# Adaptation columns 16 to 47 as matmuls, and six convolved units whose two token halves lie in neighbouring PSUM banks

## The chip, the core and the metric

One core of a Trainium2 chip runs the whole program. Its engines work side by side, each through its own queue in order: TensorE (PE, with its weight loads PEld), VectorE (DVE), ScalarE (ACT), GpSimd (POOL) and SyncE (SP), from whose queue nearly all DMAs are issued. The metric is device time in microseconds (us); lower is better.

## The reference, cut to what matters

One layer of a decoder: 1024 tokens, width 1024, float32. A conditioning vector gives six modulation vectors; the combined projection's first columns go through a short causal convolution over the tokens.

```
mod = silu(c) @ w_ada + b_ada            # 1024 -> 6 * 1024
shift1, scale1, gate1, shift2, scale2, gate2 = split(mod, 6)
h = rms_norm(x, norm1_w) * (1 + scale1) + shift1
gq, gk, gv, gz, ga, gb, sq, sk, sv = split(h @ w_in)
q, k, v = split(silu(causal_depthwise_conv(concat(gq, gk, gv), conv_w)))   # width 4
# gated delta rule on q, k, v in chunks of 64 (a triangular solve in each), gated by gz
# sliding-window attention on sq, sk, sv
x = x + gate1 * (concat(both) @ w_out)
x = x + gate2 * ffn(rms_norm(x, norm2_w) * (1 + scale2) + shift2)
```

## The kernel before

The tokens lie along the free dimension, 128 channels on the partitions. Float32 weights and activations are split into a high and a low part, and each product of a projection is three matmuls of 128x512 (`mm3`). A *unit* is one block of 128 output columns for one half of the tokens (512 columns, one PSUM bank): 8 steps of 3 matmuls. The units of all projections form one long generator, `dense`; `fill(n)` issues its next n steps. TensorE's instructions run in the order in which the program names them. The order on the other engines comes from a scheduler, which follows the program's order and prefers what stands in `high_priority`. The order of the stage is written out by hand: `VISITS_A` and `VISITS_B` say how many dense steps stand between two visits of the other work.

**The adaptation columns.** `mod` has 48 columns of 128 values. Columns 0 to 15 (shift1 and scale1) are made at the start, ahead of the first units, from `cb`, a tile that holds silu(c) on every partition. The other 32 come later: a loop of 14 rounds (`ADA_ITER`) issues six dense steps and two columns a round, and the last four come after the visit of `v3`. A column is one load of 512 KB (`load_ada`, L247) into a slot of one of the tags b, c, d, e (two slots each), and `mod_col`: on VectorE one product with a running sum (L253), or on GpSimd a product (L256) and on ScalarE a sum (L257); then VectorE adds the bias (L259). They are used far later: the first, gate1, by the output projection.

**The convolved units.** The twelve blocks of keys, queries and values (`gk`, `gq`, `gv`) go through `conv`: ScalarE reads the bank once with the newest tap (L363), VectorE adds the three older taps, shifted by 1, 2 and 3 columns (L365). Where the second half of the tokens starts, the shifted reads need the last three columns of the first half. They are kept in `tails` (L368), and three small VectorE instructions repair columns 0 to 2 (L371). The dense banks are four: two under the tag `u`, two under `sw`, which the units take in turn (`dbank`).

**What follows.** After the loop `token_gen` makes the decays (VectorE, then `psg` and `pst` on TensorE). Each of four head pairs has three visits: sums of squares from transposes (`pst_k`, `pst_q`, L708 to L711), scaled rows (`psr_k`, L721 to L727), products (`psA`, L781 to L783). `key_gen` makes the window keys (`ps_kd`). `solve` inverts all triangles on VectorE (L817, L820). Meanwhile TensorE does the values, the window queries (`ps_sq`, with rows `psr_s`) and the gates (`ps_gz`). Then come the scan, the attention, the output projection and the FFN. Most tiles of 4 KB a partition (`cb`, the keys `kn`, the values `v`, `ktok`, `vs` and others) share one pool of six slots.

## Time and profile before

| | us |
|---|---|
| median of 3 runs (1319.52 to 1326.32) | 1319.54 |
| the profiled execution | 1316.65 |
| its span, first to last instruction | 1314.9 |
| TensorE busy | 1192.7 |
| VectorE busy | 892.6 |
| GpSimd busy | 629.4 |
| ScalarE busy | 538.8 |

Busy time is the time in which at least one instruction of the engine runs. The mean granted clock of TensorE over the span is 0.96 of full speed. Times inside the profile count from the span's start.

### The profile page before, as it was taken

The numbers are of one execution on the slowest core, as the hardware profiler recorded it, in microseconds if no ns is written. First come the engines' busy times: TensorE is split into PE (matmuls) and PEld (weight loads), VectorE is DVE, ScalarE is ACT, GpSimd is POOL, SyncE is SP. The second block draws the span as 40 slices with busy tenths as digits, with TensorE's granted clock in tenths as the row PEclk, the third lists the DMA queues.
The fourth block names the chain that finished last, engine by engine and source line by source line (L and its number), as shares of the span: only waits on it lengthen the run. The fifth ranks groups of instructions, "written<-read, shape, count | busy, mean of one in ns | idle before, by whom it ended". The sixth has DMA issues, their size and how long they took to land.

```text
span 1314.9 us, 18979 instructions
## 1 busy us (share of the span) xinstructions
PE 1192.7 (91%) x6710; PEld 974.5 (74%) x6710; DVE 892.6 (68%) x1690; ACT 538.8 (41%) x1028; POOL 629.4 (48%) x453
## 2 busy tenths in 40 slices
PE   6867697896999799997998999999999999999998
PEld 5757576684788678785786788777777888888887
DVE  7999989979724677576646416877876875546430
ACT  4373555422434777434356432222232334544430
POOL 4667344534335444344354455545455545455440
PEclk8899799898999899998899999999999999999999
DMA  8727468485639865366845625556665567775651
GB/s 326 233 85 273 144 132 227 133 229 183 199 126 205 132 113 165 106 218 216 288 157 187 207 95 203 208 200 228 212 212 201 176 217 281 250 252 195 201 168 40
DMA packets 167214, 250.62 MB, mean 191 GB/s; under 512 B 40656, under 2 KB 106448, under 8 KB 165584
## 3 DMA queue, kind: packets, MB, share of 16 engines
q1 hardware_dynamic: 157520, 241.03, 56.6%
q0 software_dynamic: 9600, 8.39, 3.9%
q8 instruction: 53, 0.87, 0.3%
q14 instruction: 41, 0.34, 0.1%
HBM read 182.89 MB, written 66.45 MB: 190 GB/s over the span
## 4 chain that ended last, share of the span: by engine, by line
PE 43%; DVE 16%; DMA 8%; issue 4%; POOL 3%; ACT 3%; SPq 0%; DVEq 0%; ACTq 0%; POOLq 0%
PE ps_P L1359 5%; PE ps_P L1358 5%; PE ps_P L1360 5%; DMA wb<-in_wgate_dram 4%; PE ps_S L1358 2%; PE ps_S L1359 2%; PE ps_S L1360 2%; PE ps_c L1358 2%; PE ps_c L1359 2%; POOL wS L193 2%; PE ps_c L1360 2%; DVE wa L1427 1%; PE ps_gz L212 1%; DMA SD<-sd 1%; DVE soltmp L817 1%
## 5 line engine op out<-in xcount | busy, mean ns | idle before, releaser
L193 POOL TENSOR_TENSOR wP<-rP,wP 128x512 fp32r<-128x512 f32 (+1 forms) x84 | 108.3, 1301 | 105.3 <-ACT wP L192 100.2
L1359 PE MATMUL ps_P<-t,wP 128*128 128x512 f32 x308 | 120.4, 391 | 0.0
L1358 PE MATMUL ps_P<-t,wP 128*128 128x512 f32 x308 | 120.4, 391 | 0.0
L1360 PE MATMUL ps_P<-t,wP 128*128 128x512 f32 x308 | 120.2, 390 | 0.0
L193 POOL TENSOR_TENSOR wS<-wa,wS 128x512 fp32r<-128x512 f32 x44 | 62.8, 1437 | 111.8 <-ACT wS L192 78.9
L1360 PE MATMUL ps_S<-T,wS 128*128 128x512 f32 x264 | 102.8, 390 | 0.3 <-POOL wS L193 0.3
L1359 PE MATMUL ps_S<-T,wS 128*128 128x512 f32 x264 | 102.9, 390 | 0.0
L1358 PE MATMUL ps_S<-T,wS 128*128 128x512 f32 x264 | 102.9, 390 | 0.0
L192 ACT ACTIVATE wP<-rP 128x512 fp32r<-128x512 f32 (+1 forms) x84 | 48.4, 590 | 77.6 <-PE ps_P L1360 49.2
L1358 PE MATMUL ps_c<-B,w 128*128 128x512 f32 x176 | 70.5, 401 | 6.1 <-ACT X L1398 6.1
L1360 PE MATMUL ps_c<-B,w 128*128 128x512 f32 x176 | 69.7, 396 | 0.0
L1359 PE MATMUL ps_c<-B,w 128*128 128x512 f32 x176 | 69.7, 396 | 0.0
L1465 ACT ACTIVATE sg<-sg 128x512 f32<-128x512 f32 x33 | 20.9, 632 | 116.0 <-DVE sg L1461 116.0
L1358 PEld LDWEIGHTS ps_P<-t,wP 128*128 128x128 f32 x308 | 57.9, 188 | 12.6
L1360 PEld LDWEIGHTS ps_P<-t,wP 128*128 128x128 f32 x308 | 57.9, 188 | 12.5
L1359 PEld LDWEIGHTS ps_P<-t,wP 128*128 128x128 f32 x308 | 57.8, 188 | 12.4
L192 ACT ACTIVATE wS<-wa 128x512 fp32r<-128x512 f32 x44 | 26.7, 624 | 94.6 <-DVE wa L1426 71.8
L1424 DVE TENSOR_TENSOR ws<-wb 128x512 f32<-128x512 f32 x22 | 23.1, 1051 | 62.1 <-DMA wb<-in_wgate_dram 54.5
L1360 PEld LDWEIGHTS ps_S<-T,wS 128*128 128x128 f32 x264 | 49.6, 188 | 11.1 <-POOL wS L193 0.7
L212 PE MATMUL ps_o<-mix,w_o 128*128 128x512 f32 x128 | 53.7, 420 | 4.2 <-ACT w_o L192 4.2
L1358 PEld LDWEIGHTS ps_S<-T,wS 128*128 128x128 f32 x264 | 49.6, 188 | 10.5
L1359 PEld LDWEIGHTS ps_S<-T,wS 128*128 128x128 f32 x264 | 49.6, 188 | 10.5
(507 smaller groups left out, 3559.4 us busy)
## 6 DMA issues: line engine op xcount, KB each, us to landing
ada<-in_ada_dram SPq DMA_DIRECT2D x48, 512.0 KB, 4.7
AD<-ops SPq DMA_DIRECT2D x11, 1536.0 KB, 5.0
rP<-SD SPq DMA_DIRECT2D x16, 704.0 KB, 5.7
sd<-in_wdown_dram SPq DMA_DIRECT2D x20, 512.0 KB, 5.3
SD<-sd SPq DMA_DIRECT2D x20, 512.0 KB, 3.9
rP<-in_wdown_dram SPq DMA_DIRECT2D x12, 704.0 KB, 5.3
XD<-X SPq DMA_DIRECT2D x22, 256.0 KB, 3.3
xu<-XD SPq DMA_DIRECT2D x22, 256.0 KB, 3.4
```

The costliest lines, as they stand in the source:

```text
L192: act.activation(out=r(hi), in_=src, func=AF.Copy)
L193: last = eng.tensor_tensor(out=r(lo), in0=src, in1=hi, op=ALU.subtract)
L212: pe.matmul(out, lhsT=r(lhs[0]), rhs=r(rhs[0]), start=first, stop=False)
L817: dve.tensor_tensor(out=tv[g], in0=bc(L[:, i, i + 1:32].unsqueeze(1), (P, i, 31 - i)), in1=bc(L[:, 0:i, i:i + 1], (P, i, 31 - i)), op=ALU. ...
L1358: pe.matmul(ps, lhsT=r(wh), rhs=r(xh), start=first and i == 0, stop=False, **kw)
L1359: pe.matmul(ps, lhsT=r(wh), rhs=r(xl), start=False, stop=False, **kw)
L1360: pe.matmul(ps, lhsT=r(wl), rhs=r(xh), start=False, stop=i == n - 1, **kw)
L1424: dve.tensor_tensor(out=s1, in0=a21, in1=a22, op=ALU.add)
L1427: dve.tensor_tensor(out=a12, in0=a12, in1=a11, op=ALU.subtract)
L1465: act.activation(out=out, in_=out, func=AF.Silu)
```

## The change

The later 32 adaptation columns become matmuls in 8 groups of four columns. All 32 loads stand ahead of the loop, from a copy of the weights laid out with the 1024 inputs on the partitions (8 blocks of 128). A group (`ada_gen`) has four steps: two of 16 float32 matmuls each, then ScalarE's copy of the bank, then four matmuls of one column and VectorE's addition of four biases at once. In each product the stationary operand is 128x32, silu(c) of one block of inputs repeated over 32 columns; the four column tiles of TensorE take the blocks k = 0..3 and then k = 4..7, so a bank holds four partial rows on partitions 0, 32, 64 and 96 (each repeated 32 times). The closing matmul of a column takes the row as stationary operand and `sel`, a column that is 1 on those four partitions, and so sums the four parts and turns the row into a column. The loop keeps its 14 rounds of six dense steps; from the fourth on, three steps of the groups follow in each. The columns behind the visit of `v3` are gone.

Six of the convolved units, `gk` 3, `gq` 3 and `gv` 0 to 3, take a tile of two neighbouring banks for both token halves. They go in pairs (first half of both, then second half of both, `two_units`), and for the second half the three shifted reads of 512 columns start 1 to 3 columns ahead of its bank, in the first half's. `tails` and the repairs are not issued for them. The four dense banks are a pool of their own that is released and opened anew at two points (`switch`): ahead of these six units as two tiles of two banks, behind them as before.

```diff
+    psd = [tc.alloc_tile_pool(name="psd0", bufs=2, space=PSUM, reuse_waits="tile")]
+    def new_banks():
+        psd[0].release()
+        psd[0] = tc.alloc_tile_pool(name=f"psd{len(psd)}", bufs=2, space=PSUM, reuse_waits="tile")
+        psd.append(None)
...
+        if tag in ("u", "sw"):
+            return psd[0].tile([P, TH], F32, tag=tag, name=name)
...
+    sel = cp.tile([P, 1], F32, name="sel")
+    pool.memset(sel, 0.0)
+    for g in range(4):
+        pool.memset(sel[32 * g:32 * g + 1], 1.0)
-    def ada_some(n, tag, eng=dve):
...
+    def ada_load(tag):
+        u = ada_next[0]
+        ada_next[0] += 1
+        adat[u] = t4(f"ada{u}", (P, KT, P), tag=tag)
+        with tc.issue_after((done["kd"] if "kd" in done else done["x"]).ins):
+            sp.dma_start(out=adat[u], in_=ada2[u - 16])
+    def ada_gen(u0, q=None):
+        ps = sm(f"ps_ada{u0}", q)
+        for m in range(2):
+            for n in (2 * m, 2 * m + 1):
+                w = adat.pop(u0 + n)
+                for k in range(KT):
+                    g = k % 4
+                    pe.matmul(ps[32 * g:32 * g + 32, n * P:(n + 1) * P], lhsT=bc(c_col[:, k:k + 1], (P, 32)), rhs=w[:, k],
+                              start=k < 4, stop=k >= 4, tile_position=(0, 32 * g))
+            yield
+        row = t2(f"ada_row{u0}")
+        act.activation(out=row, in_=ps, func=AF.Copy)
+        yield
+        for n in range(4):
+            pe.matmul(ps[:, n:n + 1], lhsT=row[:, n * P:(n + 1) * P], rhs=sel, start=True, stop=True)
+        dve.tensor_tensor(out=modc[:, u0:u0 + 4], in0=ps[:, 0:4], in1=b_ada[:, u0:u0 + 4], op=ALU.add)
+        yield
...
+        if hf == 1 and ct in wides:
+            both = wides[ct].rearrange("p a t -> p (a t)")
+            for d in (1, 2, 3):
+                dve.scalar_tensor_tensor(out=out, in0=both[:, TH - d:2 * TH - d], scalar=w[:, 3 - d:4 - d], in1=out,
+                                         op0=ALU.mult, op1=ALU.add)
+            return
...
-        if hf == 0:
+        if hf == 0 and ct not in wides:
...
-    def two_units(kinds, tags):
+    def two_units(kinds, tags, wide=False):
+        if wide:
+            for kind, p in kinds:
+                wides[CT[kind] + p] = psd[0].tile([P, 2, TH], F32, tag="w", name=f"ps_{kind}{p}")
...
-                  proj("gk", 1, (1,)), proj("gq", 1, (1,)), proj("gk", 3), proj("gq", 3),
-                  *(proj("gv", p) for p in range(4)), *(proj("sq", p) for p in range(4)), proj("gz", 0, tags=("u",)), proj("gz", 1, tags=("u",)),
+                  proj("gk", 1, (1,)), proj("gq", 1, (1,)), switch(), two_units((("gk", 3), ("gq", 3)), None, True),
+                  two_units((("gv", 0), ("gv", 1)), None, True), two_units((("gv", 2), ("gv", 3)), None, True), switch(), *(proj("sq", p) for p in range(4)), proj("gz", 0, tags=("u",)), proj("gz", 1, tags=("u",)),
...
+    adas = chain(*(ada_gen(16 + 4 * i) for i in range(8)))
+    for tag in ADA_TAGS:
+        ada_load(tag)
     for i in range(ADA_ITER):
         fill(VISITS_A[0])
-        with tc.issue_after(h_done[0].ins), tc.issue_after(h_done[1].ins):
-            ada_some(1, ADA_TAGS[2 * i], pool if i not in ADA_DVE else dve)
-            ada_some(1, ADA_TAGS[2 * i + 1])
+        for _ in range(3 if i >= 3 else 0):
+            next(adas, None)
+    run(adas)
...
-        if visit is v3:
-            for i in range(32 - 2 * ADA_ITER):
-                ada_some(1, "b", pool if i % 4 else dve)
...
-        "ada": w_ada.T.reshape(48, P, D),
+        "ada": w_ada[:, 0:2 * D].T.reshape(16, P, D),
+        "ada2": tiles(w_ada[:, 2 * D:]),
```

## Rows read from the trace of the kernel before

**Rows 1.** The page: the span and TensorE's busy time, its share and instructions.
```profile
span 1314.9 us, 18979 instructions
...
PE 1192.7 (91%) x6710; PEld 974.5 (74%) x6710; DVE 892.6 (68%) x1690; ACT 538.8 (41%) x1028; POOL 629.4 (48%) x453
```

**Rows 2.** Windows: length, busy us (PE, PEld, DVE, ACT, POOL), clock, DMA.
```profile
85.00:345.00 260.00, 200.60 (x1147) 166.35 (x1145) 240.67 (x489) 109.53 (x181) 124.96 (x61) 0.89 0.60 176
345.00:1315.00 970.00, 925.95 (x5222) 751.83 (x5222) 581.13 (x1091) 388.13 (x778) 454.15 (x346) 0.98 0.60 190
...
96.90:145.70 48.80, 41.93 (x210) 36.07 (x210) 48.37 (x76) 20.73 (x46) 32.78 (x13) 0.93 0.69 248
145.70:157.70 12.00, 0.00 (x0) 0.00 (x0) 12.00 (x33) 5.58 (x9) 2.34 (x1) 0.59 0.42 131
```

**Rows 3.** Waits of TensorE up to 440 us, longest first: total, times, longest.
```profile
PE psr_s L725 <- ACT wide_s L721: 15.0, 2, 13.4
PE psg L666 <- DVE tsc L661: 12.1, 1, 12.1
PE psr_k L725 <- ACT wide_k L721: 9.9, 2, 7.5
PE ps_gk L212 <- ACT kq L387: 8.6, 1, 8.6
...
PE ps_kd L870 <- DVE aq L783: 4.0, 1, 4.0
...
PE ps_skv L212 <- DVE qt L365: 3.7, 1, 3.7
...
PE ps_skv L212 <- DVE kn L365: 2.4, 1, 2.4
```

**Rows 4.** The tile `ada`: durations in ns, min/median/max, and its loads' landing.
```profile
L256 POOL TENSOR_TENSOR ada<-ada,cb x17: 2338/2402/3221, 85.0 to 319.8; 128x1024 f32<-128x1024 f32 x17
...
L253 DVE CUSTOM_DVE_ANT_0 ada<-ada,cb x15: 1206/1211/3451, 98.6 to 306.2; 128x1024 f32<-128x1024 f32 x15
...
DMA to landing us min/median/max: 3.3/4.7/10.2
```

**Rows 5.** VectorE's groups by line between 60 and 345 us.
```profile
L371 DVE SCALAR_TENSOR_TENSOR kn<-tails,sml,kn 128x1 f32<-128x1 f32 (+2 forms) x12 | 14.4, 1202 | 0.0
...
L371 DVE SCALAR_TENSOR_TENSOR v<-tails,sml,v 128x1 f32<-128x1 f32 (+2 forms) x12 | 9.8, 812 | 0.0
L259 DVE TENSOR_TENSOR modc<-modc,sml 128x1 f32<-128x1 f32 x32 | 9.6, 314 | 0.1
```

**Rows 6.** Timeline of VectorE, modulation of the second half: start, us, what.
```profile
85.12 5.59 DVE L332 SCALAR_TENSOR_TENSOR h<-xt,modc,h 128x512 fp32r<-128x512 f32 x2
...
91.30 0.74 DVE L332 SCALAR_TENSOR_TENSOR h<-xt,modc,h 128x512 fp32r<-128x512 f32 x1
```

**Rows 7.** Timelines of GpSimd and VectorE in the solve.
```profile
311.58 5.00 POOL L256 TENSOR_TENSOR ada<-ada,cb 128x1024 f32<-128x1024 f32 x2 [10.41 <-DVE soltmp L817]
...
312.33 2.00 DVE L820 TENSOR_TENSOR lanes<-lanes,soltmp 128x234 f32<-128x234 f32 x1
314.25 2.59 DVE L817 TENSOR_TENSOR soltmp<-lanes 128x238 f32<-128x238 f32 x1
...
319.37 0.39 DVE L820 TENSOR_TENSOR lanes<-lanes,soltmp 128x238 f32<-128x238 f32 x1
```

**Rows 8.** Timelines of TensorE: float32 matmuls, stationary size, moving size.
```profile
71.22 0.95 PE L321 MATMUL ssps<-ones,sq 128*128 128x1 f32 x8
...
247.91 2.59 PE L781 MATMUL psA<-kq,kn 64*64 64x128 f32 x64
...
445.95 1.09 PE L1170 MATMUL psO<-pT,vs 128*64 128x256 f32 x8
```

**Rows 9.** Timelines of ScalarE and VectorE: the second half of `gq` 1 read out.
```profile
171.60 0.73 ACT L363 ACTIVATE qt<-ps_gq,sml 128x512 f32<-128x512 f32 x1
...
175.85 0.73 DVE L365 SCALAR_TENSOR_TENSOR qt<-ps_gq,sml,qt 128x509 f32<-128x509 f32 x1
```

More of the change, by code (lines that the diff above doesn't have):

```diff
@@ L61, in tile_hybrid_layer @@
     ada: bass.AP,
+    ada2: bass.AP,
     wmain: bass.AP,
@@ L89, in tile_hybrid_layer @@
     psp = ctx.enter_context(tc.tile_pool(name="psp", bufs=1, space=PSUM))
-    P_BUFS = {"u": 2, "sw": 2, "q0": 1, "q1": 1, "qq": 2}
+    psd = [tc.alloc_tile_pool(name="psd0", bufs=2, space=PSUM, reuse_waits="tile")]
[3 more added lines that the diff above has]
+        psd.append(None)
+    P_BUFS = {"q0": 1, "q1": 1, "qq": 2}
     def t4(name, shape=(P, T), tag=None, dt=F32):
@@ L259, in mod_col @@
             dve.tensor_tensor(out=modc[:, u:u + 1], in0=modc[:, u:u + 1], in1=b_ada[:, u:u + 1], op=ALU.add)
+    sel = cp.tile([P, 1], F32, name="sel")
+    pool.memset(sel, 0.0)
+    for g in range(4):
+        pool.memset(sel[32 * g:32 * g + 1], 1.0)
     ada_next = [16]
-    def ada_some(n, tag, eng=dve):
-        for u in range(ada_next[0], ada_next[0] + n):
-            if "kd" in done:
-                with tc.issue_after(done["kd"].ins):
-                    load_ada(u, tag)
-            else:
-                load_ada(u, tag)
-            mod_col(u, eng)
-        ada_next[0] += n
+    def ada_load(tag):
[21 more added lines that the diff above has]
+        yield
     def rstd(ps, name):
@@ L358, in tile_hybrid_layer @@
     kns, kq, vts = {}, {}, {}
+    wides, CT = {}, {"gq": 0, "gk": 4, "gv": 8}
     def conv(ps, out, ct, hf):
@@ L366, in conv @@
                                      op0=ALU.mult, op1=ALU.add)
-        if hf == 0:
+        if hf == 0 and ct not in wides:
             dve.tensor_copy(out=tails[:, ct], in_=ps[:, TH - 3:TH])
-        else:
+        elif hf:
             for d in (1, 2, 3):
@@ L423, in proj @@
         for hf in halves:
-            ps = dbank(f"ps_{kind}{p}_{hf}", tags)
+            ps = wides[CT[kind] + p][:, hf] if CT.get(kind, 99) + p in wides else dbank(f"ps_{kind}{p}_{hf}", tags)
             yield from unit(ps, w, h_hl(hf))
@@ L595, in tile_hybrid_layer, with switch @@
         w_2 = [wunit(wmain[2], "w_gk2", parts=[t4(f"w_gk2{x}", (P, KT, P), tag="e") for x in "hl"]), wunit(wmain[6], "w_gq2")]
+    def switch():
+        new_banks()
+        yield from ()
     def skv_unit(i):
@@ L1603, in tile_hybrid_layer @@
         close_pools(len(stacks[side]), side)
+    psd[0].release()
 def kernel(**inputs):
```

## The prediction

> **What bounds the kernel now.** I read the page first. TensorE works in 1192.7 us of a span of 1314.9 [rows 1], so what can be won is its idle time, and then the question is where that lies. The windows answer it: between 85 and 345 us TensorE works 200.60 of 260 us, and in the 970 us behind them 925.95 [rows 2]. The first stretch has 59.4 us of idle time and a mean granted clock of 0.89; the second is TensorE's own and moves as a block when the first gets shorter. In the first stretch VectorE works 240.67 of 260 us [rows 2]. The view of TensorE's waits names who it waits for there: a row of the pair chains or of the window queries (`psr_s` 15.0, `psr_k` 9.9), the token sums (`psg` 12.1), a bank not yet read out (`ps_gk` 8.6, `ps_skv` 3.7 and 2.4), `ps_kd` 4.0 [rows 3]. All of them end at VectorE, directly or one ScalarE instruction behind it. So the stage is a TensorE order that stands still when VectorE is late.
>
> VectorE is late for two reasons. It does adaptation columns itself: 15 of 1.2 us and the 32 additions of their bias [rows 4, 5]. And it stands still while GpSimd does the other 17, 2.4 us each [rows 4]: `L332` takes 0.74 us alone, but two of them take 5.59 us when GpSimd's column products begin in front of them [rows 6]; in the solve, instructions of 0.39 us take 2.00 and 2.59 while the products run [rows 7]. The small `L371` repairs at the half boundary suffer most: at most three columns wide, they average 1.20 us for keys and 0.81 for values, where the shortest need 0.2 [rows 5].
>
> **What the change does to the adaptation loop (88 to 158 us).** Off VectorE, GpSimd and ScalarE goes all of it: 15 products of 1.2 us, 17 of 2.4 us, and 24 of 32 bias additions. Onto TensorE go 8 groups. A group is 32 fp32 matmuls of 128 columns, and an fp32 matmul is two instructions in the trace (the 4 matmuls of `ssps` are x8 [rows 8]), so 512 passes; then 4 matmuls of one column, 8 passes.
>
> The price of a pass: `ssps`, where each must wait for the one ahead, has 8 in 0.95 us, 0.119 each [rows 8]. The passes of a group go to four column tiles in turn. No row shows a 128x32 tile, so the bounds are: one after another, 512 x 0.119 = 61 us; four at a time, 15.2 us. The nearest rows are `psA`, 64 passes of 128 columns in 2.59 us, 0.040 each, which is three times as dense as one after another; and `psO`, where the first four passes belong to one column tile and the last four to the other, and all eight, twice as wide, end within 1.09 us [rows 8]: one after another they would need 8 x 0.24 = 1.9. So column tiles run side by side, even when the program names one tile's passes first. I take four at a time with some filling and emptying: 16 steps of 32 passes, each 8 x 0.119 + 0.1 = 1.05 us, 16.8 us. By `psA`'s rate as it stands it would be 20.5.
>
> The closing columns cost 8 x 0.95 = 7.6 us at `ssps`'s price. They wait for ScalarE's copy of the bank; in two of eight groups no dense step lies between the last product, the copy and the closing matmuls, and each of those costs a full-bank ScalarE pass (0.73 us [rows 9]) and the handing over, 0.9 by estimate: 1.8. Together TensorE takes on 16.8 + 7.6 + 1.8 = 26.2 us, and nothing hides it, because it stands in TensorE's own order.
>
> Taken away in the same loop: the wait for `psg`, 12.1 us, in which TensorE does nothing at all [rows 2, 3]. The token chain that it waits for is short VectorE work behind the columns, and in the new order some 18 dense steps and twelve adaptation steps follow its inputs. The two waits of `ps_skv`, 6.1 us [rows 3], are banks not read out because VectorE is behind. Of the 8.6 us of `ps_gk` only 4.1 go (5.59 less 2 x 0.74 [rows 6]); the modulation itself stays. The clock was granted at 0.93 over the 210 matmuls of the loop [rows 2], 14% of 48.8 us at the lower of its two levels, 1.2 GHz; with the waits gone I give back 2 us. Sum 12.1 + 6.1 + 4.1 + 2 = 24.3. The loop is therefore a draw: 26.2 - 24.3 = +1.9 us.
>
> The loads are as many and as large, on the same queue, but now TensorE's order waits for them. Each slot is refilled six columns ahead; three adaptation steps and six dense steps pass in some 5 to 7 us, so a refill has about 10 us, and a load lands in 4.7 (median) to 10.2 us [rows 4]. I take no wait, with the rival below. A load that waits on SP for its slot holds the dense units' weights behind it, as it does now; the four columns that were loaded during the solve join this queue too.
>
> **The pair chains (158 to 276 us).** Six of the twelve convolved units lose their three `L371` and the copy of the tail. By rows 5 the values' 12 cost 9.8 us, and one key unit 14.4 / 4 = 3.6, one query unit about the same: 17 us of VectorE. Half of that was standing still behind GpSimd, and will partly be met by the next instruction instead. The new reads take one operand from the sums' banks, as the main sums (`L365`, 0.73 us, rows 9) do now. Besides, `cb` is no longer held after the start, so its slot of the six-slot pool is free for a key tile whose convolution waited for one. Against it stands the new wait: a pair of units owns four banks, so at the switch the first wide unit needs the bank of the unit just ahead. That is read out 5.0 us after ScalarE begins on it (171.60 to 176.58 [rows 9]). What stands behind it on TensorE is the next pair's transposes. Within the wide units the slack falls from three units to one, some 5.5 us and the visits between. The waits to win are `psr_k` and `ps_kd`, 13.9 us [rows 3]; I take 9 of them, and 4 back for the switch: -5. Bounds: -13.9 and +5.
>
> **The solve (285 to 345 us).** Four columns leave it: one VectorE product of 1.2 us and three GpSimd ones, two of which hold VectorE for 2.00 - 0.39 and 2.59 - 0.39 [rows 4, 7]; the third at their mean, 1.9. Sum 6.9 us. TensorE waits there for `psr_s` (13.4 us at the longest of 15.0 in rows 3), which hangs on the same VectorE queue, so all of it counts: -7. The second switch, to the window queries, may cost some 5 us, but the same wait covers it.
>
> **Sum:** +1.9 - 5 - 7 = -10 us. The profiled execution took 1316.65 us (span 1314.9): 1306.6. The median of the runs is 2.9 above it, which would give 1309.5; I say 1308.
>
> **Rivals.**
> *More goes than I take.* The whole 8.6 us of `ps_gk` (4.5 more), and all of 13.9 with no wait at the switch (9 more): -24, 1295. For it: VectorE is over 90% busy and loses some 30 us there. Against it: some of these chains are latency, not load.
> *The passes start strictly in order.* Then the second pass of one tile stands in front of the next tile's first, and only two run together: 512 / 2 x 0.119 = 30.5 us, 13.7 more: 1322, no change. `psO` speaks against it; `psA`'s 0.040 lies between two and four at a time. The Trainium skill (TensorE: Matmul & The Clock Gate, Part 3: Packing small matmuls) says that matmuls start and end strictly in program order; by that rule this rival holds, and the trace's `psO` does not agree.
> *The column tiles do not overlap at full height.* The rows show two column tiles of 128 rows at once, never four. One after another they cost 61 us, 44 more: 1352, slower. It decides from 0.052 us a pass on (16.8 + 10 us over 512); above 0.065 the kernel is measurably slower.
> *Banks.* The switch in full, the same at the second switch, and a short one per wide pair: 1 + 5 + 6 = 12 more: 1320. For it: VectorE's evacuations lag in this stage. Against it: the freed slot and VectorE's relief.
> *Late loads.* If half of the eight groups find a column 3 us late (landing near 10 us): 12 more, 1320. For it: GpSimd waits for these loads today; against it: the slots are asked for earlier.
>
> **How the numbers follow.** The forecast has 0.46 (own range 1301 to 1315), more gain 0.16, strict order 0.13, no overlap 0.08, banks 0.10, late loads 0.07. 0.5%, about what can be told from no change, is 6.6 us around 1319.5. Faster: nearly all of the forecast and the bigger gain, 0.60. Slower: no overlap and the upper ends of the other three, 0.15. The rest, 0.25, is no change. The range leaves out no overlap, and the ends of the others: 1291 to 1325.
>
> **What would show it.** In the loop: some 512 passes `ps_ada`, 32 in about 1 us (1.9 would be strict order, 3.8 no overlap); no wait at `psg`; TensorE at `psg` near 158 to 160 us. VectorE below 80% between 97 and 146 us. Then `psr_k` and `ps_kd` waits smaller, a new wait of a wide unit at the first switch, and no `L371` behind the third pair of units. The solve some 7 us shorter, and the block behind 345 us unchanged in length. I am wrong if TensorE waits for `ada`, if 32 passes take over 1.7 us, or if the wide units wait for banks again and again.

## The result, and the profile after

The changed kernel takes 1333.2 us (median of 10 runs, 1327.1 to 1338.5), the kernel before on the same chip 1319.5 (10 runs, 1317.3 to 1327.7). The ratio is 1.0076, with a 95% interval of 1.0049 to 1.0103: slower, by 10 us (13.7 between the medians) where 11.5 less was forecast, and outside the range.

The profiled execution took 1327.83 us. Its page, for [rows 1]: TensorE is 31.1 us busier, VectorE 47.1 less.

```profile
span 1326.0 us, 20013 instructions
...
PE 1223.8 (92%) x7286; PEld 1001.8 (76%) x7286; DVE 845.5 (64%) x1612; ACT 523.6 (39%) x1002; POOL 595.1 (45%) x441
```

The windows of the changed kernel, cut where TensorE reaches the same work as in before: the loop from `gk` 2's second half to `psg`, the pair stage, the solve part up to the scan's first `psm`, scan and output projection, the rest. Columns as in [rows 2].

```profile
93.50:168.10 74.60, 68.89 (x787) 59.17 (x788) 26.08 (x65) 19.59 (x40) 7.08 (x3) 0.91 0.60 215
168.10:285.80 117.70, 97.64 (x669) 79.95 (x668) 95.21 (x164) 55.42 (x83) 52.99 (x24) 0.94 0.62 162
285.80:358.60 72.80, 65.19 (x301) 52.75 (x299) 60.01 (x183) 20.47 (x30) 31.28 (x21) 0.93 0.69 196
358.60:653.70 295.10, 277.63 (x2394) 225.31 (x2394) 183.66 (x564) 150.59 (x357) 124.54 (x107) 0.95 0.66 169
653.70:1326.00 672.30, 643.87 (x2784) 524.09 (x2782) 402.23 (x514) 230.58 (x414) 329.58 (x236) 0.99 0.57 194
```

The same cuts in the kernel before:

```profile
96.90:157.70 60.80, 41.93 (x210) 36.07 (x210) 60.37 (x108) 26.31 (x55) 35.12 (x14) 0.86 0.63 225
157.70:276.00 118.30, 102.09 (x669) 83.86 (x670) 104.66 (x190) 57.28 (x85) 54.30 (x25) 0.91 0.62 162
276.00:353.90 77.90, 62.11 (x302) 51.22 (x301) 68.58 (x193) 22.97 (x35) 32.30 (x23) 0.91 0.66 196
353.90:648.10 294.20, 273.04 (x2394) 221.37 (x2394) 183.60 (x566) 150.52 (x357) 124.10 (x107) 0.97 0.66 173
648.10:1314.90 666.80, 644.03 (x2785) 523.22 (x2783) 392.69 (x513) 232.83 (x414) 325.59 (x236) 0.99 0.57 196
```

Read as differences: `psg` is reached 10.4 us later, the pair stage gives back 0.6 and the solve part 5.1, so the scan starts 4.7 later; scan and projection add 0.9 and the rest 5.5: 11.1 in all. VectorE tells the first half of the story. In the loop it works 26.08 of 74.60 us where it worked all of 60.80. It has been relieved, and now TensorE, 68.89 of 74.60, is the engine that everything waits for.

TensorE's waits up to 440 us, for [rows 3]:

```profile
PE ps_gk L223 <- DVE qt L412: 7.6, 1, 7.6
...
PE ps_ada L303 <- ACT ada_row L300: 5.7, 4, 2.6
PE ps_sq L225 <- POOL w_sq L204: 5.0, 1, 5.0
PE ps_gk L223 <- DVE tails L409: 4.1, 1, 4.1
PE ps_gv L223 <- DVE rsq_g L195: 3.9, 1, 3.9
...
PE ps_sq L223 <- DVE v L402: 2.1, 1, 2.1
...
PE ps_gv L223 <- DVE v L406: 1.8, 1, 1.8
```

The big waits of before (`psg`, `psr_k`, `psr_s`) are gone. New ones stand in their place, all of the changed kernel's own making: the first wide unit at the bank switch (7.6), the copies of the adaptation rows (5.7), banks of the wide `gv` units (3.9 and 1.8), and a window-query weight (5.0).

Two of them in detail. First TensorE at the column groups (timeline, columns as in [rows 8], in brackets the wait before it):

```profile
106.36 1.96 PE L296 MATMUL ps_ada<-ada,sml 128*32 128x128 f32 x64
...
113.47 1.23 PE L303 MATMUL ps_ada<-sel,ada_row 128*128 128x1 f32 x8 [1.46 <-ACT ada_row L300]
...
128.91 0.95 PE L303 MATMUL ps_ada<-sel,ada_row 128*128 128x1 f32 x8
...
142.07 1.87 PE L303 MATMUL ps_ada<-sel,ada_row 128*128 128x1 f32 x8 [2.61 <-ACT ada_row L300]
```

The 64 passes of two steps take 1.96 us, 0.031 each. In the trace they start in fours, within 0.02 us, and the next four 0.11 us later: four column tiles do run side by side. The closing matmuls cost the 0.95 us of [rows 8] when they need not wait; behind 1.46 us of waiting they take 1.23, behind 2.61 us 1.87. The granted clock in these three stretches is 1.00, 0.80 and 0.50: behind the longest wait they run at the lower of the clock's two levels, 1.2 GHz, in twice the time. ScalarE shows why the first of these copies is late, although its bank was complete:

```profile
111.30 0.69 ACT L398 ACTIVATE qt<-ps_gq,sml 128x512 f32<-128x512 f32 x1 [4.45 <-PE ps_gq L225]
111.89 1.04 ACT L203 ACTIVATE w_gq<-w_gq_1r 128x1024 fp32r<-128x1024 f32 x1
112.83 0.59 ACT L300 ACTIVATE ada_row<-ps_ada 128x512 f32<-128x512 f32 x1
```

A convolution's first pass and a weight split stand ahead of it in ScalarE's order. Second, the switch. TensorE ends `gq` 1, the newest unit, at 177.57 us, and its wait ends with that unit's last instruction on VectorE (TensorE, ScalarE, VectorE):

```profile
177.17 0.40 PE L225 MATMUL ps_gq<-h,w_gq 128*128 128x512 f32 x1
...
180.10 0.73 ACT L398 ACTIVATE qt<-ps_gq,sml 128x512 f32<-128x512 f32 x1
...
184.97 0.21 DVE L412 SCALAR_TENSOR_TENSOR qt<-tails,sml,qt 128x3 f32<-128x3 f32 x1
```

### The profile page after: what moved, and what is told of

Its sections match the earlier page's. It is cut to its first block, busy times and chain, and to the rows that moved or that the text cites. A ratio compares the mean times of both kernels' runs of the same rounds, so it can differ in the third digit from the quotient of the medians.

```text
span 1326.0 us, 20013 instructions
## 1 busy us (share of the span) xinstructions
PE 1223.8 (92%) x7286; PEld 1001.8 (76%) x7286; DVE 845.5 (64%) x1612; ACT 523.6 (39%) x1002; POOL 595.1 (45%) x441
## 4 chain that ended last, share of the span: by engine, by line
PE 54%; DVE 24%; DMA 10%; issue 4%; ACT 4%; POOL 3%; SPq 1%; DVEq 0%; ACTq 0%; POOLq 0%
PE ps_P L1406 5%; PE ps_P L1408 5%; PE ps_P L1407 5%; DMA wb<-in_wgate_dram 3%; PE ps_S L1406 2%; PE ps_S L1408 2%; PE ps_S L1407 2%; PE ps_c L1406 2%; PE ps_c L1407 2%; PE ps_c L1408 2%; DMA SD<-sd 2%; POOL wS L204 2%; DVE ada L482 2%; DVE lanes L868 1%; DVE wa L1475 1%
## 5 line engine op out<-in xcount | busy, mean ns | idle before, releaser
L204 POOL TENSOR_TENSOR wP<-rP,wP 128x512 fp32r<-128x512 f32 (+1 forms) x84 | 111.8, 1346 | 101.2 <-ACT wP L203 98.0
L1407 PE MATMUL ps_P<-t,wP 128*128 128x512 f32 x308 | 119.9, 389 | 0.0
L203 ACT ACTIVATE wP<-rP 128x512 fp32r<-128x512 f32 (+1 forms) x84 | 47.1, 587 | 65.0 <-PE ps_P L1408 32.0
L1407 PEld LDWEIGHTS ps_S<-T,wS 128*128 128x128 f32 x264 | 49.6, 188 | 10.4
L1406 PEld LDWEIGHTS ps_S<-T,wS 128*128 128x128 f32 x264 | 49.6, 188 | 10.3
```

The source lines that it names most:

```text
L203: act.activation(out=r(hi), in_=src, func=AF.Copy)
L204: last = eng.tensor_tensor(out=r(lo), in0=src, in1=hi, op=ALU.subtract)
L1406: pe.matmul(ps, lhsT=r(wh), rhs=r(xh), start=first and i == 0, stop=False, **kw)
L1407: pe.matmul(ps, lhsT=r(wh), rhs=r(xl), start=False, stop=False, **kw)
```

## Experiments

All medians are set against runs of the kernel before on the same chip; the rows without a ratio are single executions. "psg" and "scan" are the starts of these two on TensorE in the profiled execution of that kernel; that of e_ada lies 7.7 us above its median, so of e_ada only the loop is read.

| kernel | median us (before) | ratio, 95% interval | psg | scan |
|---|---|---|---|---|
| before, second profile | 1317.1 | - | 156.1 | 350.0 |
| changed, second profile | 1335.0 | - | 166.8 | 357.8 |
| e_spread, second profile | 1327.0 | - | 161.2 | 353.6 |
| e_ada | 1336.2 (1321.5) | 1.0092, 1.0056 to 1.0127 | 168.7 | 364.8 |
| e_wide | 1334.6 (1321.5) | 1.0113, 1.0072 to 1.0154 | 173.7 | 366.7 |
| e_spread | 1323.7 (1321.5) | 1.0014, 0.9992 to 1.0037 | 160.9 | 351.7 |
| e_swap | 1333.7 (1321.5) | 1.0105, 1.0071 to 1.0138 | 169.8 | 361.7 |
| e_spread_narrow | 1333.5 (1319.0) | 1.0111, 1.0081 to 1.0141 | 159.3 | 355.0 |
| e_pair | 1357.0 (1319.0) | 1.0291, 1.026 to 1.0322 | 190.6 | 380.6 |
| e_none | 1299.0 (1319.0) | 0.9842, 0.9812 to 0.9872 | 135.1 | 331.7 |
| e_half | 1333.7 (1319.0) | 1.0131, 1.0097 to 1.0166 | 164.4 | 361.3 |
| e_sw_group | 1319.9 (1320.2) | 1.0006, 0.9981 to 1.0031 | 155.9 | 348.1 |
| e_half2 | 1311.3 (1320.2) | 0.9927, 0.99 to 0.9955 | 147.2 | 342.7 |
| e_half3 | 1316.0 (1320.2) | 0.9954, 0.9932 to 0.9976 | 150.5 | 345.0 |
| e_half2_narrow | 1321.8 (1322.3) | 0.9999, 0.9974 to 1.0024 | 146.2 | 341.3 |
| e_half2_again | 1309.5 (1322.3) | 0.9899, 0.9866 to 0.9931 | 146.5 | 339.7 |

**One part at a time: e_ada and e_wide.** e_ada keeps the columns on TensorE and takes the wide pairs out:

```
-                  proj("gk", 1, (1,)), proj("gq", 1, (1,)), switch(), two_units((("gk", 3), ("gq", 3)), None, True),
-                  two_units((("gv", 0), ("gv", 1)), None, True), two_units((("gv", 2), ("gv", 3)), None, True), switch(), ...
+                  proj("gk", 1, (1,)), proj("gq", 1, (1,)), proj("gk", 3), proj("gq", 3),
+                  *(proj("gv", p) for p in range(4)), ...
```

> The adaptation columns are on TensorE as in the changed kernel; the six convolved units go through single banks with copied tails as before. Theory A (the loop became TensorE's: some 24.5 us of column matmuls, 5.7 us of waits for the row copies and slow-clock losses of 6 us stand serially where 28 us of waits stood): psg starts near 168 us as in the changed kernel (before 157.7), the pair stage is as long as before or longer (118 to 120 us), time 1.004 to 1.010 of before. Theory B (the bank switch and the wide pairs cost the time, the columns are about even): psg may be late, but the time is 0.998 to 1.002 of before.

Measured: 1.0092, psg at 168.7: theory A. The loop is late by itself, without any wide pair.

e_wide does the reverse: wide pairs and switches stay, 28 columns are done as before, the last four as one group on TensorE.

```
-    for tag in ADA_TAGS:
-        ada_load(tag)
     for i in range(ADA_ITER):
         fill(VISITS_A[0])
-        for _ in range(3 if i >= 3 else 0):
-            next(adas, None)
-    run(adas)
+        with tc.issue_after(h_done[0].ins), tc.issue_after(h_done[1].ins):
+            ada_some(1, ADA_TAGS[2 * i], pool if i not in ADA_DVE else dve)
+            ada_some(1, ADA_TAGS[2 * i + 1])
...
+    run(ada_gen(44))
```

> The wide pairs and both bank switches as in the changed kernel; columns 16 to 43 on VectorE and GpSimd in the loop as before, and only the last four, which before came inside the scan's preparation, on TensorE behind the loop, where TensorE waited 12.1 us for psg. Theory A: loop end within 2 us of before's 157.7, the solve part some 5 us shorter as in the changed kernel, time 0.993 to 0.999 of before. Theory B: the first switch waits 7 us or more again and the time is 1.003 to 1.008 of before.

Measured: 1.0113, but the edit brought a wait of its own. The four columns for TensorE shared buffers with those of VectorE and GpSimd, and TensorE stood 18.2 us for their loads; psg came at 173.7. That spoils the time. What stays readable is the switch: its wait is 7.7 us here too, whatever the loop does.

**The copies: e_spread.**

```
     for i in range(ADA_ITER):
-        fill(VISITS_A[0])
-        for _ in range(3 if i >= 3 else 0):
-            next(adas, None)
+        for _ in range(3):
+            fill(VISITS_A[0] // 3)
+            if i >= 3:
+                next(adas, None)
```

> The changed kernel with the three column steps of a place set one behind every two dense steps, so that two dense steps (1.4 us and more) lie between each row copy and its closing matmuls. Theory A: ada_row waits of 5.7 us fall under 1.5, psg starts at 162 to 165 us instead of 168, time 0.995 to 0.998 of the changed kernel (1.003 to 1.005 of before). Rival (the wait was cover for something else, h tiles or VectorE tails, that comes next): psg within 1.5 us of 168, time within 0.002 of the changed kernel.

Measured: 1.0014 of before, against 1.0076: theory A and a little more. No `ada_row` wait is left among TensorE's, psg comes at 160.9, 7.2 us earlier. Window of e_spread, from `gk` 2's second half (94.6 us here, 93.5 in the changed kernel) to psg:

```profile
94.60:160.86 66.26, 66.25 (x787) 54.29 (x788) 24.73 (x65) 18.96 (x38) 7.16 (x3) 0.97 0.67 239
```

TensorE is busy in all of it at a clock of 0.97. The changed kernel had 0.91 and 68.89 us of busy time for the same 787 matmuls: the short waits cost their own 5.7 us and, with the lower clock, 2.6 us more of busy time. Together that is 8.3 us of the loop; e_spread keeps 7.2 of them, since its loop began 1.1 us later.

**What the columns cost at all: e_none.** The edit leaves the 32 later columns out, so that the bias alone stands in their place in the modulation.

```
-    adas = chain(*(ada_gen(16 + 4 * i) for i in range(8)))
-    for tag in ADA_TAGS:
-        ada_load(tag)
+    adas = chain()
+    dve.tensor_copy(out=modc[:, 16:48], in_=b_ada[:, 16:48])
```

> e_spread with the 32 later adaptation columns left out altogether (their part of the modulation is the bias alone): no column matmuls, copies, closings or loads. It prices them. Theory A (TensorE sets the loop's end, so their 24.5 us stand on the path): psg at 136 to 142 us instead of 160.9, time 0.981 to 0.987 of e_spread. Rival (without them TensorE waits for VectorE's token sums, ready near 148 us in the changed kernel): psg at 146 to 150, time 0.988 to 0.993 of e_spread.

Measured: psg at 135.1, 0.9842 of before. Theory A, psg even a little below its bounds, and the rival's wait for the token sums did not come:

```profile
93.50:135.10 41.60, 40.70 (x210) 35.59 (x211) 21.44 (x53) 13.81 (x31) 4.79 (x2) 0.92 0.09 26
```

So the columns cost 160.9 - 135.1 = 25.8 us on TensorE, when spread (its instructions on `ps_ada` are busy for 25.7 there), and 157.7 - 135.1 = 22.6 on VectorE and GpSimd in the kernel before. That is the trade in the loop: 22.6 for 25.8, and another 7.2 for the copies in the middle. But 22.6 is for 28 columns and 25.8 for 32: it is 0.81 us a column on either side. The four that the loop took over came out of the solve part.

**The switch: e_swap and e_pair.** e_swap hands out the two buffers of a wide pair in the other order, so that the first wide unit gets the banks whose last user is older.

```
-            for kind, p in kinds:
+            for kind, p in reversed(kinds):
                 wides[CT[kind] + p] = psd[0].tile([P, 2, TH], F32, tag="w", name=f"ps_{kind}{p}")
```

> The changed kernel with the two buffers of each wide pair handed out in the other order, so that the first wide unit takes the two banks whose last user is one unit older. Theory A (the 7.6 us at the first switch is a bank that waits for the newest evacuation): that wait falls under 3 us, the second wide unit of the pair waits no more than 2 us, the pair stage is 3 to 6 us shorter than 117.7, time 0.995 to 0.998 of the changed kernel. Rival (VectorE or psr_k sets the stage's length and the wait only moves there): the stage stays within 1.5 us of 117.7 and the time within 0.002 of the changed kernel.

Measured: 1.0105. The stage, 119.0 us, keeps its length, as the rival has it, but the wait has not moved either: it is the same, and ends at the same instruction of the newest unit:

```profile
186.92 0.76 PE L223 MATMUL ps_gk<-h,w_gk 128*128 128x512 f32 x1 [7.60 <-DVE qt L412]
```

Theory A's explanation (the wrong bank) falls. What fits both is that the first tile of a new set of banks waits for the last reader of the whole old set. e_pair was to show that, with e_spread's order, the first `switch` left out and one set of two bank pairs from the start, whose halves the single units take in turn:

```
         if tag in ("u", "sw"):
+            if len(psd) == 1:
+                if pairs[1] % 2 == 0:
+                    pairs[0] = psd[0].tile([P, 2, TH], F32, tag="w", name=name)
+                pairs[1] += 1
+                return pairs[0][:, (pairs[1] - 1) % 2]
```

> e_spread with the first switch gone: from the start the banks are two pairs, single units take the halves of a pair in turn, so that the first wide unit waits for a pair whose newer unit is one unit older. Theory A (e_swap's wait stayed at 7.6 us because the first tile of a new set of banks waits for the last user of the whole old set): the 8.1 us wait falls under 3 us, the pair stage is 3 to 6 us shorter, time 0.995 to 0.999 of e_spread. Rival (VectorE sets the stage's length, and the wait comes back at psr_k or at the next bank): the stage within 1.5 us of e_spread's, time within 0.002 of it.

Measured: 1.0291. Single units in the loop now wait for whole pairs (`ps_gq` 22.6 us in five waits) and psg comes at 190.6, so the time says nothing of the switch. The pair stage does. The first wide unit starts without a wait, the second waits 0.46 us, and the wait comes back at the second half of `gk` 3, behind VectorE's last read of the first half, which ends at 221.18 us:

```profile
199.92 0.40 PE L230 MATMUL ps_gk<-h,w_gk 128*128 128x512 f32 x1
...
207.77 0.47 PE L230 MATMUL ps_gq<-h,w_gq 128*128 128x512 f32 x1 [0.46 <-DVE qt L419]
...
221.33 0.77 PE L230 MATMUL ps_gk<-h,w_gk 128*128 128x512 f32 x1 [7.84 <-DVE rsq_g L202]
```

The stage takes 119.2 us, against 117.9 in e_spread. With e_swap this speaks for the whole old set as what the first tile waits for, and it is the rival on the stage: without the wait at the switch it is no shorter.

**The wide pairs alone: e_spread_narrow**, e_spread with e_ada's edit.

> The spread-out columns of e_spread with single banks and copied tails in place of the wide pairs: beside e_spread it gives the wide pairs alone. Theory A (the wide pairs and their switches give the pair stage nothing, the first switch costing what the shorter evacuation saves, but shorten the solve part by some 5 us): psg within 1.5 us of e_spread's 160.9, the scan starts 5 to 9 us later than in e_spread, time 1.002 to 1.008 of e_spread. Theory B (the wide pairs cost time on the whole): time 0.992 to 0.998 of e_spread.

Measured: psg 159.3 (the loop takes 66.2 us in both and began 1.5 earlier here), and from there to the scan 195.7 us, against 190.8 with wide pairs: they save 4.9 us up to the scan. By the runs it is 1.0111 against 1.0014, more than that; the profiled execution is the quickest of its kernel and does not show the rest. So the wide pairs gain, against theory B. But theory A misses its ranges for the scan (3.3 us later) and the time (1.0097 of e_spread), and has the parts the wrong way round. Pair stage and solve part of e_spread_narrow:

```profile
159.30:284.00 124.70, 99.72 (x669) 81.89 (x669) 104.86 (x186) 57.05 (x85) 54.24 (x25) 0.92 0.61 157
284.00:355.00 71.00, 62.51 (x302) 51.21 (x300) 60.82 (x187) 19.64 (x29) 30.93 (x20) 0.98 0.69 189
```

In e_spread they are 117.9 and 72.9: the wide pairs shorten the pair stage by 6.8 us and lengthen the solve part by 1.9. And beside the kernel before (118.3 and 77.9), with single banks in both, the columns' move alone made the pair stage 6.4 us longer (`psr_k` waits 16.6 us, not 9.9) and the solve part 6.9 shorter. (Between two profiles of one kernel the pair stage differs by up to 2 us: 118.3 and 116.3 in before, 117.9 and 119.9 in e_spread.) One difference in the order shows: ScalarE begins to read `gk` 3 out at 201.35 us in before, behind the second pair's `wide_k`, but at 180.52 here, ahead of it, and VectorE's sums of `gk` 3 stand between the steps of that pair's chain. In before, then in e_spread_narrow:

```profile
192.88 1.15 ACT L721 ACTIVATE wide_k<-rn 128x512 f32<-128x512 f32 x2 [4.21 <-DVE rn L186]
...
201.35 1.25 ACT L363 ACTIVATE kn<-ps_gk,sml 128x512 f32<-128x512 f32 x2
```

```profile
180.52 0.73 ACT L398 ACTIVATE kn<-ps_gk,sml 128x512 f32<-128x512 f32 x1
...
200.09 1.15 ACT L769 ACTIVATE wide_k<-rn 128x512 f32<-128x512 f32 x2 [0.17 <-DVE rn L197]
```

That fits the slot of `cb`, which is free earlier now. Whether it is what makes the stage longer is not shown; no run has it alone.

**Using the wait: e_sw_group**, e_spread with the last column group in the dense order right behind the switch, buffers for it that nothing else wants there, and four more steps in `VISITS_A` for it (8 becomes 12).

```
-ADA_TAGS = "bcd" * 5 + "bcde" * 4 + "d"
+ADA_TAGS = "bcd" * 5 + "bcde" * 3 + "b" + "ccdd"
...
-                  proj("gk", 1, (1,)), proj("gq", 1, (1,)), switch(), two_units((("gk", 3), ("gq", 3)), None, True),
+                  proj("gk", 1, (1,)), proj("gq", 1, (1,)), switch(), ada_gen(44), two_units((("gk", 3), ("gq", 3)), None, True),
```

> e_spread with the last group of four columns moved from the end of the loop to the first bank switch, where TensorE waits 8.1 us; 28 columns stay in the loop. Theory A (columns cost time only where TensorE has no wait to put them in): psg 3 us earlier (157 to 159 us), the switch wait down by some 3 us to 4 to 6 us, scan start 2.5 to 4 us earlier than 351.7, time 0.997 to 0.999 of e_spread. Rival (the switch wait ends with VectorE's last tail, which moves with the loop's end, and the wait keeps its length): wait still 7.5 to 8.5 us behind the group, scan start within 1 us.

Measured: psg 155.9, scan 348.1, 3.6 us earlier than e_spread, and 1.0006 of before, which e_spread's 1.0014 can't be told from. The wait of 8.1 us shrinks to these, of which the first is the group's own, for its bank:

```profile
PE ps_ada L296 <- ACT kd L762: 2.0, 1, 2.0
PE ps_ada L303 <- ACT ada_row L300: 1.0, 1, 1.0
PE ps_gk L223 <- DVE qt L406: 0.9, 1, 0.9
```

That is theory A's way, but of the 3.6 us 2.4 are an earlier start of the loop (92.2 against 94.6 us). The loop itself is 2.6 us shorter, and from psg to the scan it takes 192.2 us, 1.4 more than in e_spread: at the wait the group cost about half of what it cost in the loop, not nothing.

**Dividing the columns: e_half, e_half2, e_half3.** If 28 columns on VectorE and GpSimd cost 22.6 us and 32 on TensorE 25.8, on different engines, each side should take half. In e_half TensorE has four groups in the loop, and the other engines take a column each in eight of its places:

```
+        for j in range(3):
+            fill(VISITS_A[0] // 3)
+            if i >= 2 and j < 2:
+                next(adas, None)
+            if j:
+                u = next(vec, None)
+                if u is not None:
...
+                        load_ada(u, next(tags))
+                        mod_col(u, pool if j == 1 else dve)
```

> Half and half: columns 16 to 31 on TensorE, two steps in each place, one behind two dense steps; columns 32 to 47 on VectorE and GpSimd in the first eight places of the loop; wide pairs as in e_spread. Theory A (the loop's time is that of the fuller engine: all on VectorE 157.7, all on TensorE 160.9 when spread): psg at 148 to 154 us, time 0.991 to 0.996 of e_spread, 0.992 to 0.998 of before. Rival (loads or the buffers of both kinds hold the loop): psg at 157 or later, time within 0.003 of e_spread.

Measured: the rival. psg 164.4, 1.0131; TensorE waited 18.2 us for loads, whose buffers were given out in one row to both kinds. e_half2 gives TensorE's columns buffers of their own, loads them four ahead, leaves VectorE and GpSimd twelve, and puts one group at the switch as e_sw_group does:

```
+    adas = chain(*(ada_gen(16 + 4 * i) for i in range(4)))
+    tags, vtags = iter("bc" * 16), iter("de" * 16)
...
+    for i in range(ADA_ITER):
+        for j in range(3):
+            fill(VISITS_A[0] // 3)
+            if i >= 2 and j < 2:
...
+                next(adas, None)
...
+            if j:
+                vec_col(pool if j == 1 else dve)
```

> e_half had TensorE wait 18.2 us for column loads, whose buffers were those of VectorE's columns. Here 16 columns on TensorE in the loop and four at the first switch, with buffers of their own, twelve on VectorE and GpSimd in the first places of the loop. From e_none (psg at 135.1 with no columns, none of it waiting for VectorE) and e_spread (160.9 with 32): 16 columns on TensorE give 148, 12 on VectorE and GpSimd 12/28 of the 22.6 us that 28 put between 135.1 and before's 157.7, 145. Theory A (fuller engine): psg at 147 to 151 us, time 0.988 to 0.994 of before. Rival (loads again): a wait for column loads over 4 us, psg at 154 or later, time 0.996 to 1.003 of before.

Measured: psg 147.2, 0.9927; again, on another chip, 146.5 and 0.9899. Theory A: it beats both kernels, with the wait for loads down to this:

```profile
PE ps_ada L296 <- DMA ada<-in_ada_dram: 3.1, 2, 2.3
```

e_half3 has `range(3)` for `range(4)`, and so 16 columns on VectorE and GpSimd.

> As e_half2 with 12 columns on TensorE in the loop, four at the switch, 16 on VectorE and GpSimd. Theory A: TensorE's part gives 135.1 + 12 x 0.8 = 145, the other engines' 135.1 + 16/28 x 22.6 = 148; psg at 146 to 150 us, time within 0.003 of e_half2. Rival (loads, or VectorE's tails that wait behind its columns): psg at 153 or later.

Measured: psg 150.5 behind a wait of 5.2 us for the token sums, 0.9954. With 16 columns TensorE waits for VectorE again. By the runs e_half3 and e_half2 can't be told apart (the intervals overlap), so where the best division lies is open.

Last, e_half2 once more beside a form of it with single banks (e_ada's edit; the column group stays where the switch was), on one chip:

> e_half2 again beside its narrow form on one chip. Theory A (its gain is psg 10 us earlier than in before and a scan start 7 to 11 us earlier): 0.990 to 0.995 of before and faster than the narrow form by 0.002 to 0.006. Rival (its gain was one chip's): 0.996 or more.

> e_half2 with single banks and copied tails in place of the wide pairs; the last column group stands where the switch was. Theory A (the wide pairs are worth the 5 us that they saved between psg and the scan in e_spread against e_spread_narrow): psg within 1.5 us of 147.2, the scan starts 2 to 6 us later than in e_half2 (342.7), time 0.994 to 0.999 of before. Rival (with the columns divided, VectorE's tails hide in the loop and the wide pairs save nothing): scan start within 1 us of e_half2's, time 0.990 to 0.994 of before.

Measured: 0.9899 for e_half2, 0.9999 for its narrow form. psg to scan is 195.1 us narrow and 193.2 to 195.5 wide, so up to the scan the wide pairs save little here (the scan starts 1.6 us later than in e_half2_again): near the rival, whose time is nonetheless far off, as theory A's is. The wide form is 12 us quicker by the medians. In these two profiles 8.0 of it lie behind the scan's start, in 2394 TensorE instructions that are the same in both. The windows from the scan to the end of the output projection, narrow first, then wide:

```profile
341.30:652.00 310.70, 289.23 (x2394) 235.75 (x2394) 181.40 (x565) 150.89 (x357) 124.15 (x107) 0.91 0.64 163
```

```profile
339.70:642.40 302.70, 283.24 (x2394) 231.36 (x2394) 183.37 (x565) 150.65 (x357) 124.03 (x107) 0.93 0.64 165
```

Both are longer than before's 294.20 and at a lower clock than its 0.97. Why the narrow form has it lower still is open.

**The later blocks: before_again and after_again, e_spread_again.** The scan's clock first.

> The kernel before, unchanged, for a second profile. In its shown profile the granted clock stays at 1.00 between 62 and 94 us behind the scan's first matmul but for one window, where all profiles of changed kernels so far fall to 0.5 to 0.8 there and take 3 to 6 us longer for the same instructions. Theory A (a chance of the execution, not of the change): this execution falls there too, or is at 1320 us and more elsewhere. Rival (the wait that the change took out of the solve part keeps the clock up in before): the clock stays at 1.00 there again and the stretch takes 145 us.

Measured: theory A. Windows of 8 us, 72 to 96 us behind the scan's first matmul, in the first profile of before and then in the second:

```profile
425.90:433.90 8.00, 6.60 (x94) 5.68 (x95) 5.84 (x33) 7.95 (x34) 4.36 (x6) 1.00 1.28 217
433.90:441.90 8.00, 6.12 (x76) 4.51 (x76) 6.47 (x26) 7.66 (x22) 2.05 (x3) 1.00 0.06 10
441.90:449.90 8.00, 7.44 (x89) 6.15 (x86) 7.01 (x31) 6.49 (x20) 5.36 (x8) 1.00 0.97 253
```

```profile
422.00:430.00 8.00, 6.62 (x83) 5.72 (x83) 5.30 (x32) 7.95 (x34) 4.30 (x6) 0.80 1.21 210
430.00:438.00 8.00, 7.92 (x55) 5.94 (x54) 5.32 (x24) 6.43 (x19) 0.40 (x2) 0.77 0.09 14
438.00:446.00 8.00, 7.29 (x83) 7.13 (x84) 5.13 (x15) 5.67 (x18) 7.01 (x9) 0.65 0.64 192
```

The same kernel: once the clock holds, once it falls, and scan and projection take 294.2 or 298.2 us. The first profile of before had reached the scan 3.9 us later and made it good here.

> The changed kernel again, for a second profile. Theory A (the later block goes with the execution, by its granted clock and its loads): the stretch from the end of the output projection to the end takes 665 to 670 us here. Rival (it goes with the kernel): 671 to 674 us again. The loop is as before in both: psg at 167 to 169 us, 7.6 us at the switch, 5.7 us for the row copies.

> e_spread again, for a second profile. Theory A (execution): the stretch behind the output projection takes 665 to 670 us; rival (kernel): 672 to 675 again, as in its first profile (673.4).

Measured: the rival in both, the last block goes with the kernel. It took 672.3 and 679.0 us in the changed kernel, 673.4 and 675.0 in e_spread, but 666.8 and 667.1 in before and 665.4 and 665.9 in e_half2. One wait marks it, VectorE's for the gate weights from 640 us on, in before, changed kernel and e_half2:

```profile
DVE ws L1424 <- DMA wb<-in_wgate_dram: 54.5, 11, 7.0
```

```profile
DVE ws L1472 <- DMA wb<-in_wgate_dram: 57.0, 11, 8.1
```

```profile
DVE ws L1493 <- DMA wb<-in_wgate_dram: 53.0, 11, 7.2
```

In the eight profiles with the short block (665 to 669 us) it is 49.6 to 55.0 us, in the ten with the long one (672 to 679) 56.2 to 59.3. That is a mark, not the whole of it: the blocks lie further apart than the waits. Which of the two a kernel gets follows neither part of the change: e_wide, with 28 columns on VectorE and GpSimd, has the long block (675.3), e_half2, with 20 on TensorE and wide pairs, the short. What makes these loads land later is open.

## Why the prediction was wrong, step by step

Of some 21 us between the forecast span (10 less) and the measured one (11.1 more), 8.5 lie in the loop, 4.4 in the pair stage, 1.9 in the solve part, 0.9 in scan and output projection and 5.5 behind.

- **A draw in the loop (+1.9): the first step that failed.** The mechanism was right. The two large terms were near: the passes with the closings were put at 24.4 us, and e_none and e_spread give 25.8; what could be taken away was put at 24.3, and e_none shows 22.6. That is 3.1 of the 8.5 us between +1.9 and +10.4. The other 5.4 are the small terms. The copies: two waits of 0.9 were counted, by looking for places with no dense step between, and there were four of 1.4 on average, because ScalarE's queue holds other work; 5.7 against 1.8. And the clock: 2 us were to be given back "with the waits gone", but with the new waits it was 0.91 in the loop against 0.93 in before, and beside e_spread that is 2.6 us of busy time (the loop began 1.1 us earlier than e_spread's, which takes the sum of 6.5 to 5.4). e_spread, without both, reaches `psg` 3.2 us behind before.
- **The pair stage (-5): failed, -0.6.** The step that failed is a term put at nothing: that the stage without wide pairs would be as long as before, once VectorE has no columns. e_spread_narrow shows 124.7 us against 118.3, +6.4. The prediction counted the freed slot of `cb` as relief; the difference in order shown above fits that slot, and works the other way. The wide pairs then gave 6.8 where -5 was forecast: near in size, but not by the terms, for the waits of `psr_k` that they took away were 16.6 us and the switch cost 7.6, not 4. The read-out of the newest unit took 5.1 us, as in [rows 9]; ScalarE began it 2.5 us after the unit's end, behind its passes of the pair chain, and no transposes were left for TensorE to do meanwhile. The wide `gv` units waited another 3.9 and 1.8 for their banks. That was the rival "banks", right in place, with a chance of 0.10; but e_pair, without the wait at the switch, has no shorter stage.
- **GpSimd's standstill moved on.** The tails left, and the next small instruction stood still instead, as the prediction said half of it would: in the changed kernel a 32-column product of 0.19 us takes 4.61 while GpSimd does a product of 4.74, and the read-out behind it is late, which is the 3.9 us of `ps_gv`. VectorE, then GpSimd:

```profile
227.08 4.61 DVE L195 TENSOR_TENSOR rsq_g<-rsq_g 128x32 f32<-128x32 f32 x1
231.61 0.73 DVE L406 SCALAR_TENSOR_TENSOR v<-ps_gv,sml,v 128x511 f32<-128x511 f32 x1
```

```profile
226.90 4.74 POOL L838 TENSOR_TENSOR kq<-kq,egrow 128x2048 f32<-128x2048 f32 x1 [1.16 <-PE psA L829]
```

- **The solve (-7): right, -5.1** (77.9 to 72.8; 77.6 to 72.5 in the second profiles). The columns' leaving is worth the forecast: with single banks the part is 71.0 us long, -6.9. The wide pairs cost 1.9 of it. `psr_s`'s 13.4 us went; 5.0 came back as the wait for the weights `w_sq`, whose GpSimd split is late (1.4 in e_spread_narrow), and 2.1 at the second switch, which I had taken as covered.
- **The block behind 345 us "unchanged in length": failed.** Its instructions are unchanged, but the part behind the output projection is 5.5 us longer (11.9 in the second profiles). Shown: it goes with the kernel, and with the gate weights' landing. Not shown: why.
- **Rivals.** No overlap is out, and so is strict order at its price: 64 passes took 1.96 us, where it was put at 3.8. That price, 0.119 a pass, was the weak point: the prediction took `ssps` for passes that wait for each other, but its rows are passes of one column that start 0.11 us apart and each last 0.25. Eight full-width passes of 128 columns (`pst_k`) take 1.03 us in the changed kernel, 0.13 each, which bears the price out for passes of this length. The Trainium skill (TensorE: Matmul & The Clock Gate, Part 3: Packing small matmuls) has matmuls start and end strictly in program order. Passes that start four at a time do not agree with that if the two passes of a matmul stand next to each other in TensorE's order; no record names its tile, so this stays an inference. Late loads did not come in the changed kernel (0.4 us), but they did in e_wide and e_half, once both kinds of column shared buffers.
- **The base.** The profile of before lies 2.9 us under its median, which I had allowed for. It kept the clock up in the scan, but the second profile, which did not, took about as long (1317.1): the clock there is not shown to be the reason.

## What to carry to other kernels

Moving work from the engine that is late to the one that waits pays only up to the length of the waits, and the move makes the other engine the bound: price the removal by leaving the work out (22.6 us here for 28 columns) and the addition the same way (25.8 for 32), and if they are near each other, divide the work. Dividing took about 1% off in both forms: from 1.0014 to 0.993 and 0.990 with wide pairs, from 1.0111 to 1.000 with single banks. Price a second change with the first one in place, too: the wide pairs had to make good 6.4 us of pair stage that the columns' move had cost. A short cross-engine round trip in the order of a busy TensorE cost more than its length here, 5.7 us of waits and 2.6 of busy time at a lower clock; put dense steps in between, and put loose work at the waits that can't be removed (the 8.1 us at the switch took a group of columns at about half its price). Buffers that two engines' work share in one row can tie the faster to the slower: TensorE waited 18.2 us for loads in e_half, and 3.1 in e_half2, which is 2% quicker; e_half2 also loads further ahead, has four columns fewer on the slower side and a group at the switch, so the buffers' part alone is not shown.

## What the runs showed of the hardware

- Four 128x32 column tiles of float32 matmuls run side by side: 64 passes of 128 columns took 1.96 us, 0.031 each, against 0.13 for full-width passes of as many columns (`pst_k`, 8 in 1.03 us).
- The same eight one-column passes took 0.95 us without a wait ahead, 1.23 behind 1.46 us and 1.87 behind 2.61, at granted clocks of 1.00, 0.80 and 0.50.
- The first unit on a newly opened set of banks waited 7.6 us for the newest reader of the old set, whichever of the new buffers it took (e_swap), and not at all where no new set was opened (e_pair).
- The scan's 2394 TensorE instructions, the same in all kernels, took 294 (before) to 311 us (e_half2_narrow) at a mean granted clock of 0.97 to 0.91; between two profiles of the kernel before the difference was 4.0 us. An earlier start need not arrive in full: e_half2 starts the scan 7.3 us before the second profile of before on the same chip, and ends the projection 6.0 before it.
- Gate-weight loads of the same size in the same queue order land so that VectorE waits 50 to 59 us for them, by kernel; the cause is open.
